# A one-core mixture-of-experts layer: residual placed in PSUM at the router, gate applied at the down-projection copies, gathers moved into gaps

## The chip, the cores and the metric

The kernel runs on one core of one Trainium2 chip, as one program. A core has a matrix engine (TensorE, PE in the rows; PEld is its weight load), VectorE (DVE), ScalarE (ACT), GpSimd (POOL) and SyncE (SP), which issues nearly all transfers here, and 16 DMA engines that move weights from HBM into SBUF. Matmuls write only into PSUM, which has eight banks of 512 fp32 columns. The metric is the device time of one execution in microseconds (us), as the median of several runs. The profile is of one execution.

## The reference

One transformer layer over 256 latent positions and 256 context positions of width 1024: a modulated RMS norm, a mixing stage (Fourier group, neighbourhood attention, short convolution, one output projection), then a mixture of experts with 32 experts of width 512, two per token out of one group of eight, and a final norm. What the change touches is the last part:

```python
x = x + g1 * mix_out(fx, attn_x, conv_x, w_fourier, w_out)
hx2 = rms_norm(x, norm2) * (1 + sc2) + sh2
y = hier_moe(hx2.reshape(-1, d), w_rg, b_rg, w_re, b_re, w_gate, w_up, w_down)
x = x + g2 * y.reshape(b, n, d)          # g2: one gate per column
return rms_norm(x, norm_final)
# in hier_moe, for every expert e:
he = jax.nn.silu(t @ w_gate[e]) * (t @ w_up[e])
y = y + combine[:, e:e + 1] * (he @ w_down[e])
```

## The kernel before

**Stages.** Up to about 175 us the mixing stage runs. Then the router (lines 781 to 836) computes logits, picks two experts per token, ranks tokens within each expert with five small matmuls (lines 829 to 832) and builds one-hot matrices. Then 32 experts follow in order, in eight groups of four. Up to 32 tokens of an expert (CAP) are computed; a branch (`overflow`, line 978) holds the rest.

**Weights.** Each expert has three transfers of 2 MB: `gu0`, `gu1` (the two halves of the contraction of gate and up) and `dn`. They land in slabs: ten in `slabs` and an eleventh, `more`, opened where the first stage's memory is closed (line 842). `pump` (line 123) issues the next transfers of a list on SyncE's queue as soon as the program order has a free slab; the transfer itself waits until the slab's last reader is done. `drop` gives a slab back: `gu0` and `gu1` of an expert within `hidden` (line 925), `dn` after the down projection (line 945). With eleven slabs, the transfer for `gu1` of expert 4 waits for `dn` of expert 0.

**One expert** (`expert`, line 954). `hidden` runs 32 gate/up matmuls in eight steps j (line 922; a matmul shows as two records, so 64), four for `gu0` and four for `gu1`. In step 7 `gather` (line 890) fetches the next expert's tokens: a one-hot matmul (line 897), a copy, two transposes (line 902), and the norm's gain and shift (line 906, VectorE). Then Silu (line 930, ScalarE), the product (line 932, VectorE), a transpose (line 934) and a copy. `project_down` (line 939) runs 16 matmuls (line 944) and copies the result into rows 32i of `yg`, four copies that alternate between VectorE and ScalarE (line 952). The next group's first gather is not in a step 7: it stands after `scatter`.

**Combine weights.** In the first expert, between `hidden` and `project_down`, `weights` (line 850) computes the two softmaxes' weights on VectorE and ScalarE. `weighted(g)` (line 878) multiplies a group's one-hot by them on GpSimd and transposes the result on TensorE (line 885). All engines run their own instructions in program order, so `project_down` stands behind this transpose on TensorE.

**Collecting.** `scatter(g)` (line 908) adds a group's four expert outputs into `yp`, four PSUM banks that hold the sum over all groups but the last, without the residual and without the gate g2.

**The end.** The last group is written out by hand (lines 1030 to 1075). The three gathers of experts 29 to 31 run ahead of expert 28. After its down projection VectorE multiplies `yp` by the gate and adds it to the residual `xs` (lines 1045, 1046, four times each). Identity matmuls (line 1053) put `xs` into four other banks, `py`. `group_add` (line 1069) adds experts 28 to 30 there, around the gate/up matmuls of expert 31. Then expert 31's output is added in five pieces, and the final norm and the store follow (lines 1100 to 1130). The last `gu1` comes in four pieces, the last `dn` in five.

Of the kernel before, what the change touches and what calls it, by code (L numbers as in the profile page):

```python
# [23 lines left out]
P = 128  # L24
# [53 lines left out]
def tile_kernel(ctx: ExitStack, tc: tile.TileContext, x, cx, small_a, small_b, b_g1, b_g2, w_ada, w_in, w_out, w_gu, w_dn, out):  # L78
# [746 lines left out]
    pr = [bank((P, NE)) for _ in range(3)]  # L825
    for fs in zip(route(0), route(1)):
        for f in fs:
            f()
    PE.matmul(pr[0], trib, msk[:, 0, :], start=True, stop=True)
    for i, first_ in ((1, trib), (2, onesb)):  # L830
        PE.matmul(pr[i], onesb, msk[:, 0, :], start=True, stop=False)
        PE.matmul(pr[i], first_, msk[:, 1, :], start=False, stop=True)
    for fs in zip(place(0, pr[0]), place(1, pr[1])):
        for f in fs:
            f()
    DVE.tensor_reduce(most, pr[2], axis=AX.X, op=OP.max)
    pro.close()
    over = keep.tile([P, 1], I32, name="over")
    ge = keep.tile([P, 2, NG], F32, name="ge")


# [7 lines left out]

    def weights():  # L850

        DVE.tensor_scalar(over, most, float(CAP), None, op0=OP.is_gt)
        for t in range(2):
            DVE.tensor_scalar(sm[:, t, 1:2], mg[:, t, 0:1], -1.0, None, op0=OP.mult)
            ACT.activation(ge[:, t, :], gl[:, t, 0:4], AF.Exp, bias=sm[:, t, 1:2], scale=1.0, accum_out=sm[:, t, 2:3])
        DVE.tensor_tensor(sm[:, :, 6:7], me[:, :, 1:2], me[:, :, 0:1], OP.subtract)
        ACT.activation(sm[:, :, 7:8], sm[:, :, 6:7], AF.Exp)
# [7 lines left out]
    yp = [mbank() for i in range(4)]  # L865
    state = {}
    onehots = {}

    def group(g):

        st = fst if g == 0 else onehot(g, mo.tile([P, 2, 4, CAP], F32, name="st"))
        onehots[g] = st
        sr = fsr if g == 0 else mo.tile([P, 2, 4, CAP], F32, name="sr")
        if g:
            DVE.tensor_tensor(sr, st, rr[:, :, None, None].to_broadcast([P, 2, 4, CAP]), OP.mult)
        state[g] = [mo.tile([P, 4, NJ, CAP], F32, name="xg", tag="xg"), None, None, sr]

    def weighted(g):

        st = onehots[g]  # L880
        sw = mo.tile([P, 2, 4, CAP], F32, name="sw", tag="sw")
        POOL.tensor_tensor(sw, st, cmb[:, :, 4 * g:4 * g + 4, None].to_broadcast([P, 2, 4, CAP]), OP.mult)
        pg = mbank((P, 2, P))
        for t in range(2):
            PE.transpose(pg[:, t, :], sw[:, t], ident)
        sl = mo.tile([P, 2, P], F32, name="sl", tag="sl")
        ACT.copy(sl, pg)
        state[g][1:3] = sl, mo.tile([P, D], F32, name="yg", tag="yg")

    def gather(e):  # L890

        g, i = divmod(e, 4)
        xg, sr = state[g][0], state[g][3]
        pg = mbank((P, 256))
        for t in range(2):
            for q in range(4):
                PE.matmul(pg[32 * q:32 * q + 32, :], sr[:, t, i, :], xs[:, t, blk(q, 256)], start=(t == 0), stop=(t == 1))  # L897
        gt = mo.tile([P, 256], F32, name="gt", tag="sw")
        (DVE.tensor_copy if e % 2 else ACT.copy)(gt, pg)  # L899
# [3 lines left out]
        dst = xg[:, i].rearrange("p (q c) n -> p c q n", c=2)  # L903
# [4 lines left out]
    def scatter(g):  # L908

        _, sl, yg, _ = state[g]  # L910
        for t in range(2):
            for h in range(2):
                PE.matmul(yp[2 * t + h], sl[:, t, :], yg[:, blk(h, 512)], start=(g == 0), stop=(g == NE // 4 - 2))  # L913

    def hidden(e, fill={}, work=None):
        g, i = divmod(e, 4)
        xg = state[g][0]
        wgu = [loaded[f"gu{h}", e].rearrange("p (s j f) -> p s j f", s=2, j=4) for h in range(2)]
        pg = mbank((P, 2, P))
        for j in range(NJ):  # L920
            for q in range(4):
                PE.matmul(pg[32 * q:32 * q + 32], xg[:, i, j, :], wgu[j // 4][:, :, j % 4, q * P:(q + 1) * P],  # L922
# [4 lines left out]
            for k in fill.get(j, ()):  # L927
                work(k)
# [3 lines left out]
        DVE.tensor_tensor(hh, pg[:, 1, :], sg, OP.mult)  # L932
        pt = mbank((P, P))
        PE.transpose(pt, hh, ident)  # L934
        ht = mo.tile([P, P], F32, name="ht", bufs=2)
        DVE.tensor_copy(ht, pt)
        return ht

    def project_down(e, ht, yg, i):
# [7 lines left out]
        for q in range(4):  # L947
            dst, src = yg[32 * i:32 * i + 32, blk(q, 256)], pd[32 * q:32 * q + 32, :]
            if e >= NE - 4:
                DVE.tensor_tensor(dst, src, g2b[32 * i:32 * i + 32, blk(q, 256)], OP.mult)  # L950
            else:
                (ACT.copy if q % 2 else DVE.tensor_copy)(dst, src)  # L952

    def expert(e):
        g, i = divmod(e, 4)
        ht = hidden(e, {NJ - 1: (e + 1,)} if i < 3 else {}, gather)
        if i == 0:
            if g == 0:
                weights()
            weighted(g)  # L960
        project_down(e, ht, state[g][2], i)

# [15 lines left out]
    def overflow():  # L978
# [3 lines left out]
        for t in range(2):  # L982
# [7 lines left out]
            for e in range(NE):  # L990
                gu = w_gu[e].rearrange("h p (s j f) -> p h s j f", s=2, j=4)
                dn = w_dn[e].rearrange("p (q k f) -> p q k f", q=4, k=4)
                for k in range(4):
# [10 lines left out]
                    for q in range(4):  # L1004
# [6 lines left out]
                        PE.matmul(yp[2 * t + q // 2][:, blk(q % 2, 256)], ident, y, start=False, stop=False)  # L1011

    fst = mo.tile([P, 2, 4, CAP], F32, name="st")
    group(0)
    gather(0)
    onehot(0, fst)
    for e in range(NE - 4):
        expert(e)
        g, i = divmod(e, 4)
        if i == 3:  # L1020
            scatter(g)
            if g == 3:
                n_over = nc.values_load(over[0:1, 0:1], min_val=0, max_val=1)
                with tc.If(n_over > 0):  # L1024
                    overflow()
# [192 lines left out]
```

## Time and profile before

| what | us |
|---|---|
| median of three runs (641.08 to 642.42) | 641.42 |
| the profiled execution's own time | 643.3 |
| its span, first to last instruction | 641.4 |
| TensorE busy | 486.1 (76%) |
| VectorE busy | 234.8 (37%) |
| ScalarE busy | 142.2 (22%) |
| 16 DMA engines, SyncE's queue | 92.1% of the span |
| mean rate of all transfers | 384 GB/s |
| mean granted TensorE clock | 0.917 |

All stages count into the shares. The rate over 40 slices and the rows of a stage tell more than a share of the whole. Chains and waits are inferred from semaphore events. Some matmul records can be missing.

### The profile page before, as it was taken

To read this page: it belongs to the slowest core of one execution; us is meant where nothing else is said; L and a number is where in the kernel's file an instruction comes from. 1 tells how busy PE (TensorE), PEld (TensorE's weight loads), DVE (VectorE), ACT (ScalarE), POOL (GpSimd) and SP (SyncE) were. 2 spreads that over 40 slices of the span, in tenths; PEclk is the share of its full clock that TensorE was granted. 3 is DMA by queue.
4 is the path that set the end of the run, shared out by engine and by line. 5 is a ranking of instruction groups with operands and counts; after the bars stand their busy time and mean duration, and the time that the engine had idled before them with its cause. 6 is when DMAs were issued, how large, how long until landed. Compare 5 with 4: busy or idle time off the path is not lost.

```text
span 641.4 us, 11767 instructions
## 1 busy us (share of the span) xinstructions
PE 486.1 (76%) x5133; PEld 294.5 (46%) x5133; DVE 234.8 (37%) x552; ACT 142.2 (22%) x319; POOL 10.3 (2%) x24
## 2 busy tenths in 40 slices
PE   3899999999966787777866665766766757578685
PEld 3788885856743344334423232432423333225342
DVE  5959785797642222222211111211211111122423
ACT  4564345756312111011101000101010000001003
POOL 1000000000000000000000000000000000000000
PEclk9999999999967889899889788987987898888798
DMA  8999973499997999999999999999999999999961
GB/s 344 424 424 407 394 300 131 145 376 396 391 391 298 429 425 427 425 425 424 427 427 424 427 425 419 426 425 428 425 424 426 427 427 427 425 427 424 420 230 65
DMA packets 21222, 246.16 MB, mean 384 GB/s; under 512 B 2214, under 2 KB 3242, under 8 KB 6956
## 3 DMA queue, kind: packets, MB, share of 16 engines
q1 hardware_dynamic: 21016, 245.08, 92.1%
q8 instruction: 42, 0.69, 0.4%
q10 hardware_dynamic: 148, 0.27, 0.1%
q14 instruction: 16, 0.13, 0.1%
HBM read 244.28 MB, written 1.05 MB: 383 GB/s over the span
## 4 chain that ended last, share of the span: by engine, by line
PE 46%; DMA 43%; DVE 7%; ACT 2%; issue 2%; POOL 0%; DVEq 0%; ACTq 0%; POOLq 0%; SPq 0%
DMA gu<-in_w_gu 24%; DMA dn<-in_w_dn 18%; PE b L524 12%; PE m L922 8%; PE m L944 5%; PE b L722 4%; PE m L897 2%; PE m L913 2%; PE b L664 1%; PE b L709 1%; DVE xg L906 1%; PE b L699 1%; DVE a L293 1%; PE b L310 1%; PE m L902 1%
## 5 line engine op out<-in xcount | busy, mean ns | idle before, releaser
L922 PE MATMUL m<-gu,xg 128*32 128x256 f32 x2048 | 132.1, 409 | 39.9 <-DMA gu<-in_w_gu 33.0
L922 PEld LDWEIGHTS m<-gu,xg 128*32 128x32 f32 x2048 | 70.8, 118 | 97.5 <-DMA gu<-in_w_gu 35.9
L944 PE MATMUL m<-dn,ht 128*32 128x256 f32 x992 | 82.3, 489 | 16.0 <-DMA dn<-in_w_dn 7.3
L944 PEld LDWEIGHTS m<-dn,ht 128*32 128x32 f32 x992 | 38.4, 136 | 47.8 <-issue 32.0
L952 DVE COPY yg<-m 32x256 f32<-32x256 f32 x56 | 23.4, 418 | 99.7 <-PE m L944 87.4
L952 ACT COPY yg<-m 32x256 f32<-32x256 f32 x56 | 20.4, 363 | 158.1 <-DVE yg L952 158.1
L524 PE MATMUL b<-uh,ws 128*128 128x256 f32 (+1 forms) x240 | 51.8, 306 | 0.0
L906 DVE TENSOR_TENSOR xg<-m,a 128x256 f32<-128x256 f32 x32 | 13.6, 425 | 83.0 <-PE m L902 83.0
L524 PEld LDWEIGHTS b<-uh,ws 128*128 128x128 f32 x240 | 39.1, 188 | 4.8 <-issue 2.8
L930 ACT ACTIVATE sg<-m 128x128 f32<-128x128 f32 x32 | 8.9, 278 | 125.3 <-PE m L922 125.3
L934 PE MATMUL m<-ident,hh 128*128 128x128 f32 x32 | 10.1, 314 | 35.1 <-DVE hh L932 35.1
L524 PE MATMUL b<-ul,ws 128*128 128x256 f32 (+1 forms) x120 | 35.8, 301 | 0.0
L899 DVE COPY gt<-m 128x256 f32<-128x256 f32 x16 | 6.8, 425 | 78.8 <-PE m L897 78.8
L897 PE MATMUL m<-xs,sr 128*32 128x256 f32 x448 | 31.7, 402 | 4.5 <-PEq L1024 4.5
L913 PE MATMUL m<-yg,sl 128*128 128x512 f32 x56 | 25.9, 605 | 6.5 <-ACT yg L952 6.5
L902 PE MATMUL m<-ident,gt 128*128 128x128 f32 x64 | 14.3, 307 | 19.0 <-DVE gt L899 10.8
L932 DVE TENSOR_TENSOR hh<-m,sg 128x128 f32<-128x128 f32 x32 | 9.1, 285 | 53.6 <-ACT sg L930 53.6
L495 ACT CAST ws<-in 128x1024 fp32r<-128x1024 f32 x20 | 21.0, 1049 | 33.2 <-PE b L524 30.7
L524 PE MATMUL b<-ws,uh 128*128 128x512 f32 (+1 forms) x96 | 26.2, 361 | 1.9 <-ACT uh L353 1.9
L722 PE MATMUL b<-ws,cat 128*128 128x512 f32 x96 | 27.4, 414 | 0.0
L500 DVE TENSOR_TENSOR ws<-in,ws 128x1024 fp32r<-128x1024 f32 x20 | 24.3, 1222 | 7.7 <-ACT ws L495 7.5
L934 PEld LDWEIGHTS m<-ident,hh 128*128 128x128 f32 x32 | 4.5, 140 | 45.2 <-issue 28.8
(249 smaller groups left out, 561.1 us busy)
## 6 DMA issues: line engine op xcount, KB each, us to landing
gu<-in_w_gu SPq DMA_DIRECT2D x63, 2048.0 KB, 39.2
dn<-in_w_dn SPq DMA_DIRECT2D x31, 2048.0 KB, 39.2
ada<-in_w_ada SPq DMA_DIRECT2D x12, 2048.0 KB, 12.6
in<-in_w_in SPq DMA_DIRECT2D x3, 2048.0 KB, 9.9
in<-in_w_in SPq DMA_DIRECT2D x8, 512.0 KB, 15.9
out<-in_w_out SPq DMA_DIRECT2D x2, 2048.0 KB, 9.5
gu<-in_w_gu SPq DMA_DIRECT2D x4, 512.0 KB, 28.5
dn<-in_w_dn SPq DMA_DIRECT2D x3, 512.0 KB, 11.5
```

The lines of the kernel that those rows point to most:

```text
L495: ACT.copy(ws[:, 0], loaded[kind, i][:, blk(c, 1024)])
L500: DVE.tensor_tensor(split[n][:, 1], loaded[kind, i][:, blk(c, 1024)], split[n][:, 0].bitcast(F32), OP.subtract)
L524: PE.matmul(po, st, mv, start=begins, stop=(c == 3 and tail and not any(po is v[1] for v in todo[n + 1:])))
L722: PE.matmul(held["yo", t, h], held["cat"][:, a, MIX[n], blk(t)], ws[:, b, h, :], start=(held["nm", t, h] == 0), stop=(held["nm", t, h] == ...
L897: PE.matmul(pg[32 * q:32 * q + 32, :], sr[:, t, i, :], xs[:, t, blk(q, 256)], start=(t == 0), stop=(t == 1))
L902: PE.transpose(pt[:, c], gt[:, blk(c)], ident)
L906: DVE.tensor_tensor(dst, src, w, op)
L913: PE.matmul(yp[2 * t + h], sl[:, t, :], yg[:, blk(h, 512)], start=(g == 0), stop=(g == NE // 4 - 2))
L922: PE.matmul(pg[32 * q:32 * q + 32], xg[:, i, j, :], wgu[j // 4][:, :, j % 4, q * P:(q + 1) * P], start=(j == 0), stop=(j == NJ - 1))
L934: PE.transpose(pt, hh, ident)
L944: PE.matmul(pd[32 * q:32 * q + 32, :], ht[:, 32 * k:32 * k + 32], wdn[:, q, k, :], start=(k == 0), stop=(k == 3))
L952: (ACT.copy if q % 2 else DVE.tensor_copy)(dst, src)
```

## The change

1. The four result regions `py` are opened at the router. Identity matmuls put the residual `xs` into them there, ahead of the five ranking matmuls. `yp` is gone: `scatter` adds straight into `py`.
2. The first stage's memory and banks are closed after the logits' first step, ahead of the rest of the routing.
3. The exponentials of the combine weights move to the router, as do two activations that load the tables of Exp and Silu. The rest of `weights` moves ahead of expert 0.
4. The gate g2 is laid out once (`g2q`, four one-row matmuls and a copy). The four copies after a down projection become four VectorE multiplications by it.
5. `gather` is cut in two: `gathered` (one-hot matmuls and the copy) runs after the gate/up matmuls, where Silu and the product are being computed; `placed` (transposes, gain and shift) runs after the hidden state's transpose. This holds at group borders too, but for expert 16, which stands behind the overflow branch.
6. `weighted` runs in a group's second expert, its transposes (`turned`) in the third; `scatter(g - 1)` runs in the first expert of group g. In the last group the update of `xs`, the late identity matmuls, the three early gathers and an extra one-hot product with its transposes are gone.

The diff, cut to its core:

```diff
+    routes = route(0), route(1)
+    for fs in routes:
+        fs.pop(0)()
     pro.close()
+    ACT.activation(sm[:, :, 3], zero.to_broadcast([P, 2]), AF.Exp)
...
+    py = {}
+    for a, b in ((0, 512), (512, 768), (768, 1024)):
+        whole = mbank((P, 2, 256)) if a else None
+        for t in range(2):
+            py[t, a, b] = whole[:, t, :] if a else mbank()
+            PE.matmul(py[t, a, b], ident, xs[:, t, a:b], start=(t == 0 or not a), stop=False)
+    pr = mbank((P, 3, NE))
+    for fs in zip(*routes):
+        for f in fs:
+            f()
+    PE.matmul(pr[:, 0, :], trib, msk[:, 0, :], start=True, stop=True)
...
+    for t in range(2):
+        DVE.tensor_scalar(sm[:, t, 1:2], mg[:, t, 0:1], -1.0, None, op0=OP.mult)
+        ACT.activation(ge[:, t, :], gl[:, t, 0:4], AF.Exp, bias=sm[:, t, 1:2], scale=1.0, accum_out=sm[:, t, 2:3])
+    DVE.tensor_tensor(sm[:, :, 6:7], me[:, :, 1:2], me[:, :, 0:1], OP.subtract)
+    ACT.activation(sm[:, :, 7:8], sm[:, :, 6:7], AF.Exp)
+    ACT.activation(sm[:, :, 3:4], sm[:, :, 6:7], AF.Silu)
...
-    yp = [mbank() for i in range(4)]
...
+        for (t, a, b), p in py.items():
+            PE.matmul(p, sl[:, t, :], yg[:, a:b], start=False, stop=False)
...
-            if e >= NE - 4:
-                DVE.tensor_tensor(dst, src, g2b[32 * i:32 * i + 32, blk(q, 256)], OP.mult)
-            else:
-                (ACT.copy if q % 2 else DVE.tensor_copy)(dst, src)
+            rows = blk(q, 32)
+            DVE.tensor_tensor(yg[blk(i, 32), blk(q, 256)], pd[rows, :], g2q[rows, :], OP.mult)
+
+    def upto(e):
...
+        return hidden(e, {NJ: [fetch], NJ + 1: [put]})
 
     def expert(e):
         g, i = divmod(e, 4)
-        ht = hidden(e, {NJ - 1: (e + 1,)} if i < 3 else {}, gather)
+        ht = upto(e)
+        if i == 2 and g < NE // 4 - 1:
+            group(g + 1)
         if i == 0:
-            if g == 0:
-                weights()
-            weighted(g)
+            if g not in (0, 4):
+                scatter(g - 1)
+            state[g][2] = mo.tile([P, D], F32, name="yg", tag="yg")
         project_down(e, ht, state[g][2], i)
+        if i == 1:
+            state[g][1] = weighted(g)
+        if i == 2:
+            pg = turned(g, state[g][1])
...
+    g2q = mo.tile([P, 256], F32, name="g2q")
...
     onehot(0, fst)
+    weights()
...
     gate_rows()
+    expert(NE - 3)
     gain_rows()
-    project_down(NE - 4, ht, yg, 0)
-    for t in range(2):
-        for h in range(2):
-            hs = blk(h, 512)
-            DVE.tensor_tensor(junk, yp[2 * t + h], g2b[:, hs], OP.mult)
-            DVE.tensor_tensor(xs[:, t, hs], xs[:, t, hs], junk, OP.add)
...
-    for k in (0, 1, 2):
-        group_add(k)
-    ht = hidden(e, {6: (3,), 7: (4, 5)}, group_add)
+    expert(NE - 2)
...
+    ht = hidden(e, {3: [partial(group_add, k) for k in (0, 1, 2)], 6: [partial(group_add, 3)], 7: [partial(group_add, k) for k in (4, 5)]})
```

## Rows read from the trace of the kernel before

**Rows 1.** The page, part 2: DMA engines' busy tenths and rate, 40 equal slices.

```profile
DMA  8999973499997999999999999999999999999961
...
GB/s 344 424 424 407 394 300 131 145 376 396 391 391 298 429 425 427 425 425 424 427 427 424 427 425 419 426 425 428 425 424 426 427 427 427 425 427 424 420 230 65
```

**Rows 2.** Timeline, SyncE's transfer issues, 190 to 210 us; columns: start, duration, operation, count.

```profile
191.55 0.33 SPq L152 DMA_DIRECT2D dn<-in_w_dn  x1
...
194.48 11.49 SPq L152 DMA_DIRECT2D gu<-in_w_gu  x2
```

**Rows 3.** Busy time by stretch, 202 to 208 us: PE, PEld, DVE, ACT, POOL, clock, DMA.

```profile
202.00:204.00 2.00, 2.00 (x21) 0.92 (x24) 0.00 (x0) 0.37 (x1) 0.00 (x0) 0.50 0.54 229
...
204.00:206.00 2.00, 2.00 (x24) 0.96 (x20) 0.35 (x1) 0.00 (x0) 0.00 (x0) 0.50 0.04 16
...
206.00:208.00 2.00, 2.00 (x30) 0.92 (x24) 0.48 (x2) 0.73 (x2) 0.00 (x0) 0.64 0.71 156
```

**Rows 4.** Timeline, TensorE and one VectorE row, router to first down projection; brackets: idle before.

```profile
177.16 2.87 PE L778 MATMUL b<-sa,x1t 128*128 128x40 f32 x24
...
180.07 0.26 DVE L788 SCALAR_TENSOR_TENSOR lg<-b,cst,lb 128x40 f32<-128x40 f32 x1 [1.29 <-PE b L778]
...
182.22 0.19 PE L829 MATMUL b<-msk,trib 128*128 128x32 bf16 x1 [2.19 <-DVE msk L796]
...
183.71 1.94 PE L897 MATMUL m<-xs,fsr 128*32 128x256 f32 x16 [1.12 <-DVE cst L836]
...
187.85 6.56 PE L922 MATMUL m<-gu,xg 128*32 128x256 f32 x64 [0.98 <-DVE xg L906]
...
201.33 0.69 PE L885 MATMUL m<-ident,sw 128*128 128x128 f32 x2 [3.48 <-POOL sw L882]
...
201.95 3.64 PE L944 MATMUL m<-dn,ht 128*32 128x256 f32 x32
```

**Rows 5.** Timeline, TensorE, one scatter and two neighbouring experts, 236 to 262 us.

```profile
236.19 3.70 PE L913 MATMUL m<-yg,sl 128*128 128x512 f32 x8 [0.93 <-ACT yg L952]
...
252.21 3.66 PE L922 MATMUL m<-gu,xg 128*32 128x256 f32 x64
...
255.67 1.07 PE L897 MATMUL m<-xs,sr 128*32 128x256 f32 x16
...
261.42 3.64 PE L922 MATMUL m<-gu,xg 128*32 128x256 f32 x64
```

**Rows 6.** Timeline, the last group's residual update and the last gate/up matmuls.

```profile
593.99 0.69 DVE L1045 TENSOR_TENSOR fin<-m,fin 128x512 f32<-128x512 f32 x1
...
599.44 4.27 PE L1053 MATMUL m<-xs,ident 128*128 128x512 f32 x9
...
624.85 0.64 PE L922 MATMUL m<-gu,xg 128*32 128x256 f32 x8
```

**Rows 7.** Last weights: issues, median us to landing (page and 594 to 598 us), DMA end.

```profile
gu<-in_w_gu SPq DMA_DIRECT2D x63, 2048.0 KB, 39.2
...
572.61 0.33 SPq L152 DMA_DIRECT2D gu<-in_w_gu  x1
...
592.17 5.60 SPq L150 DMA_DIRECT2D gu<-in_w_gu  x1
...
gu<-in_w_gu SPq DMA_DIRECT2D x1, 512.0 KB, 25.0
...
620.00:622.00 2.00, 2.00 (x32) 1.13 (x34) 0.00 (x0) 0.00 (x0) 0.00 (x0) 1.00 0.42 116
```

**Rows 8.** Timeline, TensorE: two gate/up halves after a wait for their transfer.

```profile
497.50 3.62 PE L922 MATMUL m<-gu,xg 128*32 128x256 f32 x32 [2.00 <-DMA gu<-in_w_gu]
...
542.67 1.93 PE L922 MATMUL m<-gu,xg 128*32 128x256 f32 x32 [2.10 <-DMA gu<-in_w_gu]
```

**Rows 9.** The copies out of the down projection: the page's group, and the last group's.

```profile
L952 DVE COPY yg<-m 32x256 f32<-32x256 f32 x56 | 23.4, 418 | 99.7 <-PE m L944 87.4
...
592.20 1.76 DVE L950 TENSOR_TENSOR yg<-m,fin 32x256 f32<-32x256 f32 x4 [7.03 <-PE m L944]
```

More of the change, by code (lines that the diff above doesn't have):

```diff
@@ L885, in weighted, with gathered @@
             PE.transpose(pg[:, t, :], sw[:, t], ident)
[L886 to L893, printed above, removed]
+        state[g][1] = mo.tile([P, 2, P], F32, name="sl", tag="sl")
+        ACT.copy(state[g][1], pg)
+        return pg
+    def gathered(e):
         pg = mbank((P, 256))
@@ L908, in scatter, with hidden @@
     def scatter(g):
-        _, sl, yg, _ = state[g]
-        for t in range(2):
-            for h in range(2):
[L913 to L917, printed above, removed]
+        _, sl, yg = state[g]
+        for (t, a, b), p in py.items():
+            PE.matmul(p, sl[:, t, :], yg[:, a:b], start=False, stop=False)
+    def hidden(e, between={}):
         wgu = [loaded[f"gu{h}", e].rearrange("p (s j f) -> p s j f", s=2, j=4) for h in range(2)]
@@ L926, in hidden @@
                 pump()
-            for k in fill.get(j, ()):
-                work(k)
+            for f in between.get(j, ()):
+                f()
         sg = mo.tile([P, P], F32, name="sg", tag="sg", bufs=2)
@@ L1010, in overflow, with tokens @@
                         DVE.tensor_scalar(y, pd, late[:, t, e:e + 1], None, op0=OP.mult)
-                        PE.matmul(yp[2 * t + q // 2][:, blk(q % 2, 256)], ident, y, start=False, stop=False)
+                        pd = mbank((P, 256), "f")
+                        PE.matmul(pd, ones[32 * q:32 * q + 1, :], rg[32 * q:32 * q + 1, :], start=True, stop=True)
+                        DVE.tensor_tensor(y, y, pd, OP.mult)
+                        p = py[(t, 0, 512) if q < 2 else (t, 256 * q, 256 * q + 256)]
+                        PE.matmul(p[:, blk(q, 256)] if q < 2 else p, ident, y, start=False, stop=False)
+    def tokens():
+        return mo.tile([P, 4, NJ, CAP], F32, name="xg", tag="xg")
     fst = mo.tile([P, 2, 4, CAP], F32, name="st")
+    xg = tokens()
     group(0)
-    gather(0)
+    placed(0, gathered(0))
+    g2q = mo.tile([P, 256], F32, name="g2q")
+    pq = mbank((P, 256))
+    for q in range(4):
+        PE.matmul(pq[blk(q, 32), :], ones[32 * q:32 * q + 1, 0:32], rg[32 * q:32 * q + 1, :], start=True, stop=True)
+    ACT.copy(g2q, pq)
     onehot(0, fst)
+    weights()
     for e in range(NE - 4):
         expert(e)
[L1019 to L1025, printed above, removed]
-            group(g + 1)
-            gather(e + 1)
-    g = NE // 4 - 1
-    weighted(g)
-    _, sl, yg, _ = state[g]
-    for i in (1, 2, 3):
-        gather(NE - 4 + i)
-    ht = hidden(NE - 4)
+        if e == 15:
+            scatter(3)
+            n_over = nc.values_load(over[0:1, 0:1], min_val=0, max_val=1)
+            with tc.If(n_over > 0):
+                overflow()
+            xg = tokens()
+            placed(e + 1, gathered(e + 1))
+    g = NE // 4 - 1
+    expert(NE - 4)
     fin = take("fin")
@@ L1039, in tile_kernel @@
     gate_rows()
+    expert(NE - 3)
     gain_rows()
[L1041 to L1063 removed]
+    expert(NE - 2)
+    _, sl, yg = state[g]
     e = NE - 1
```

86 lines of the change are left out of this document (37 added, 49 removed).

## The prediction, made before the changed kernel was run

> **What bounds the kernel now.** I read the rate of transfers first. From about 208 us to 610 us the DMA engines are busy and move 419 to 429 GB/s [rows 1], and nothing in the change makes a transfer smaller. So TensorE work between these times has no price of its own; what counts is where the stream stops and what is left when it ends. At 80 to 130 us it is low as well, but the change touches nothing there.
>
> The stop is at 202 to 208 us: the DMA share is 0.54, 0.04 and 0.71 in three stretches of 2 us [rows 3], idle time of (0.46 + 0.96 + 0.29) x 2 = 3.4 us. SyncE's row shows why: it issues two transfers from 194.48 on, and the second gets out only after 11.49 us, at 206.0 [rows 2]. That is `gu1` of expert 4, which needs the slab of `dn` of expert 0, and expert 0's down projection ran from 201.95 to 205.6 [rows 4]. Two things make it late. Expert 0's gate/up matmuls took 6.56 us [rows 4] where the same 64 records take 3.66 later on [rows 5], and the one-hot matmuls before them 1.94 (16 records) against 1.07: the granted clock was at its lower level (1.2 GHz). And TensorE stood idle for 3.48 us in front of the transposes of line 885 [rows 4], since the combine weights weren't ready.
>
> At the other end TensorE runs behind the stream. The last quarter of `gu1` of expert 31 was issued at 592.17 and landed 25.0 us later, at 617.2 [rows 7]; its matmuls start at 624.85 [rows 6], 7.65 us after. The check: `gu0` of expert 31, issued at 572.61, lands by the median of 39.2 us at 611.8, and a 2 MB transfer takes 4.9 us at 426 GB/s, so its `gu1` is in by about 617; the stream runs out at 620 to 622 [rows 7]. From 624.85 to the end of the span are 16.55 us of a chain that the change leaves as it is.
>
> **Part by part: the router.** The residual's identity matmuls stream 2 x 512 + 4 x 256 = 2048 columns, as a scatter does, which takes 3.70 us at the higher clock [rows 5]; at the lower clock it would be 7.4, and nine of the twelve records of line 1053 took 4.27 us there [rows 6]. They stand behind the last logits matmul, which ends at 180.03. Their banks are free when the last logits are read, at 180.33 at the latest [rows 4]. Before, TensorE waited from 180.03 to 182.22 for VectorE's routing, so 2.2 us of them are hidden. The ranking matmuls stand behind them: they move from 182.22 to 184.0, a loss of 1.8 us, or up to 5.5 at the lower clock. I take the former, since TensorE was busy without a gap until 180.03 [rows 4] and now has no pause there.
>
> Then the five ranking matmuls, VectorE's placing and the one-hot matmuls follow as before: 183.71 - 182.22 = 1.5 us later the gather starts [rows 4], at 185.5. If the clock holds it takes 1.07 instead of 1.94. The way from the gather's end to the gate/up matmuls was 187.85 - 185.65 = 2.2 us, with transposes at the lower clock; I take 2.0. Expert 0 starts at 188.6, 0.7 us later than before, but ends its gate/up matmuls at 192.2 against 194.4. No wait for combine weights follows: their last VectorE steps are done beside these matmuls. Of the gap's work (gather of expert 1 1.07, transposes) I count 2 us, then 1.9 for the down projection. `dn` of expert 0 is free at about 196.2 instead of 205.6. The stream runs dry at about 203 [rows 3], and 0.7 us pass between the issue at 206.0 and the flow. So there are some 6 us to spare, and even with all of it at the lower clock (start 192, gate/up 6.6, 3.3 in the gap, 3.6) it is free at 205.5, which is as before. **The stop of 3.4 us goes.** By bytes (229 + 16 + 156 GB/s where 426 was possible) it is 4.1; I take 3.4, as packets under way at the restart are counted late. All later landings come 3.4 us earlier.
>
> Closing the first stage's memory earlier moves the eleventh slab in program order only: its transfer waits for the last reader, the logits matmuls, either way. I cost it at nothing; 0 to 1 us would be covered by the queue that is full then.
>
> **The middle.** One expert takes 261.42 - 252.21 = 9.2 us of TensorE's time [rows 5], against 3 x 4.92 = 14.8 us of its transfers. Each edit is inside the 5.6 us between: the gathers in the gap hide 1.07 us behind Silu and the product (a gain that the wait for the next weights swallows); the four copies by VectorE alone take 1.76 us as multiplications [rows 9], 0.44 each, where VectorE's copies took 0.42 [rows 9] and alternated with ScalarE one after the other; the scatter, now behind the next group's first gate/up matmuls, puts 3.70 us ahead of that expert's down projection, so its slab comes free 3.7 us later, with eight transfers queued ahead. ScalarE loses half of these copies, which frees nothing that others wait for. All cost 0.
>
> **The end.** Gone from TensorE's way are eight VectorE operations at 0.69 us [rows 6], 5.5 us, the identity matmuls, 4.27 us of which followed them [rows 6], and the burst of early gathers. So TensorE can follow the landings. `gu0` of expert 31 is in at 611.8 - 3.4 = 608.4. Its 32 records take 1.93 us at the higher clock and 3.62 at the lower; after a wait of 2 us both happen [rows 8]. Then three group additions, now 512 + 512 + 256 columns: 1280/2048 x 3.70 = 2.3 us. Steps 4 to 6 take 3 x 0.48, the addition in step 6 0.46. So the last step starts at 608.4 + 1.93 + 2.3 + 1.45 + 0.46 = 614.5, or at 616.2 with the first half at the lower clock; the piece itself is in at 617.2 - 3.4 = 613.8, so TensorE sets it by 0.7 to 2.4 us. I take 615.2, between the two, since both clocks occur after such a wait. The last `dn` piece is in by about 622 - 3.4 = 618.6 and is wanted 7.5 us after that step starts, later than it lands. End of the span: 615.2 + 16.55 = 631.8 us.
>
> **A rule against it.** In the end of before the clock stood at its higher level (1.00 at 620 to 622 [rows 7]), with TensorE busy and behind; after the change it waits for transfers in the last expert. [...]
>
> **The rivals.**
> (1) *Cold end.* The last expert from `gu0` on at 1.2 GHz: 608.4 + 3.6 + 4.6 + 2.9 + 0.9 = 620.4 for the last step, less what the clock regains while TensorE is then busy without a gap; with the final chain slower by 1 us at most half of it holds: about 635. For it: the waits. Against: after 608 TensorE has hardly a pause.
> (2) *The stop stays.* Identity matmuls at the lower clock and a cold expert 0 free `dn` at 205.5, as worked out: 631.8 + 3.4 = 635.2. Against: TensorE is warm when they start.
> (3) *No gain at the end.* The landing at 617.2 is one row; were the last `gu1` quarter in only when the stream ends (622), the slack would be 2.9 us instead of 7.65, giving 641.4 - 3.4 - 2.9 = 635.1; with the stop kept too, 638.5. If the residual's update had not been what the last expert waited for, the same.
> (4) *Slower.* The gap's serial order (gate/up, gather, transpose, copy, transposes, down projection) with three rotating banks makes an expert longer than its transfers. The point is 14.8 us. At the higher clock matmuls are 3.66 + 1.07 + 0.44 + 0.30 + 1.93 = 7.4 of the 9.2 us; all at the lower clock it would be 16.6 us, 1.8 over, and over 28 experts some 50 us more: about 690. Just past the point, at 14.9 to 15.2, the loss eats the gain of 9.6 us and the time is 642 to 645. Against: matmul busy time leaves 5.6 us of air, and TensorE catches up with the stream in before [rows 5, 8].
>
> **How the numbers follow.** The three runs' median, 641.42, is equal to the profiled span, 641.4; that execution's own time, 643.3, is 1.9 above. Gains are taken off the median: 641.42 - 3.4 - 6.2 = 631.8 (on the profiled execution 633.7). Chances: forecast 0.70, (1) 0.10, (2) 0.07, (3) 0.09, (4) 0.04. Lower end: 4.1 us for the stop, no lateness of TensorE: 641.4 - 4.1 - 7.65 = 629.6, and 0.6 for the landing read from one row: 629.0. Upper end: rivals 1 to 3, 635.2, and the clock's share: 636.0. Differences of 0.2% (1.3 us) are what a measurement of this kernel can tell. Of (3) a third ends near no change: same 0.04, slower 0.04, faster 0.92.
>
> **What would show it.** In the changed profile: no stretch around 202 to 208 us with a low DMA share; expert 0's gate/up matmuls in about 3.7 us and starting near 188.6; identity matmuls at 180.3 to 184; the down projection of expert 0 done by about 197; experts 28 to 31 each waiting for a transfer; the last gate/up step at 614 to 616, and 16 to 17 us behind it. The prediction is wrong if the stop stays, if TensorE still doesn't wait for transfers in the last group, or if the final chain grows beyond 18 us at the lower clock.

## The result and the profile after

The changed kernel took 635.62 us (633.13 to 636.62) against 641.92 for the kernel before in the same set: a ratio of 0.989 [0.986, 0.993], a gain of 6.3 us where 9.6 were forecast. Two more sets of the same file gave 634.71 against 642.53, 0.988 [0.985, 0.991], and 634.39 against 641.16, 0.988 [0.986, 0.991]. The profiled execution took 636.62 us; its span is 634.8, beside a span of 641.4 before.

The rate of transfers comes first: page of the changed kernel, part 2, 40 equal slices, to be laid beside [rows 1].

```profile
DMA  9999983399999999999999999999999999999981
GB/s 358 418 423 405 392 320 132 134 355 393 392 390 381 427 424 424 427 424 428 422 427 427 426 427 422 422 424 425 427 426 425 425 426 427 425 427 424 422 309 70
```

The slice that had 298 GB/s has 381. The stretches of [rows 3], in the changed kernel (busy us of PE, PEld, DVE, ACT, POOL, then granted clock, DMA share, GB/s):

```profile
202.00:204.00 2.00, 1.87 (x30) 1.14 (x34) 1.02 (x3) 0.08 (x1) 0.00 (x0) 1.00 1.01 422
204.00:206.00 2.00, 2.00 (x44) 1.19 (x40) 1.46 (x4) 0.00 (x0) 0.00 (x0) 1.00 0.98 418
206.00:208.00 2.00, 2.00 (x44) 1.23 (x40) 0.22 (x1) 0.05 (x1) 0.00 (x0) 1.00 1.02 434
```

The stop is gone. TensorE's way from the router to the first down projection (timeline of the changed kernel; beside [rows 4]):

```profile
180.35 5.41 PE L846 MATMUL m<-xs,ident 128*128 128x512 f32 x12 [0.35 <-DVE lg L788]
185.59 0.18 PE L851 MATMUL m<-msk,trib 128*128 128x32 bf16 x1
...
186.87 1.07 PE L905 MATMUL m<-xs,fsr 128*32 128x256 f32 x16 [1.00 <-DVE fsr L823]
...
189.96 3.66 PE L932 MATMUL m<-gu,xg 128*32 128x256 f32 x64 [0.46 <-PE m L1063]
...
195.33 1.93 PE L958 MATMUL m<-dn,ht 128*32 128x256 f32 x32
```

The residual's matmuls (line 846) took 5.41 us, not 3.70: in the windows at 180 to 182 and 182 to 184 us the granted clock is 0.62 and 0.52. The ranking matmuls therefore come 3.4 us later than before. All the same the down projection is done at 197.3, since the rest runs at the higher clock and no wait for weights is left.

The end (timeline of the changed kernel, beside [rows 6]; brackets show the wait):

```profile
564.70 1.93 PE L932 MATMUL m<-gu,xg 128*32 128x256 f32 x32 [2.79 <-DMA gu<-in_w_gu]
571.05 3.64 PE L932 MATMUL m<-gu,xg 128*32 128x256 f32 x32 [4.42 <-DMA gu<-in_w_gu]
...
610.39 3.53 PE L932 MATMUL m<-gu,xg 128*32 128x256 f32 x32 [2.31 <-DMA gu<-in_w_gu]
613.85 2.46 PE L1095 MATMUL m<-yg,sl 96*128 96x512 f32 x6
...
618.31 0.64 PE L932 MATMUL m<-gu,xg 128*32 128x256 f32 x8
```

TensorE now waits for transfers in the last group, so it follows the stream instead of running behind it. The last gate/up step starts at 618.31, where 615.2 was forecast, and 634.8 - 618.31 = 16.5 us stand behind it, as forecast (16.55). Of the 3.1 us, 2.0 are there when `gu0` of expert 31 lands, at 610.39 instead of 608.4; the other 1.1 are mostly its matmuls at the lower clock, 3.53 us, where I had taken a value between the two levels.

SyncE's issues tell the pace of landings, as it gets a transfer out when an earlier one is in (the issue at 571.07 beside the wait that ends at 571.05). Timeline of SyncE, changed kernel:

```profile
559.71 0.33 SPq L152 DMA_DIRECT2D gu<-in_w_gu  x1
564.62 0.33 SPq L152 DMA_DIRECT2D dn<-in_w_dn  x1
571.07 0.33 SPq L152 DMA_DIRECT2D gu<-in_w_gu  x1
```

The steady step is 4.90 us. Here one is 6.45: a landing is 1.55 us late, while the DMA share stays at 1.00 from 566 to 572 us. In this profile that happens at 228, 347, 442 and 571 us, and at 403, where the next step makes it up; in the profile before, with about 1.05 us each, at 314, 409 and 528. So the issue of `gu0` of expert 31, at 572.61 [rows 7], comes 1.54 us earlier and not 3.4.

### The profile page after: what moved, and what is told of

Read it like the earlier page. It is cut to its first block, busy times and chain, and to the rows that moved or that the text cites. A ratio compares the mean times of both kernels' runs of the same rounds, so it can differ in the third digit from the quotient of the medians.

```text
span 634.8 us, 11800 instructions
## 1 busy us (share of the span) xinstructions
PE 484.0 (76%) x5167; PEld 298.1 (47%) x5167; DVE 247.7 (39%) x587; ACT 128.0 (20%) x281; POOL 9.1 (1%) x20
## 3 DMA queue, kind: packets, MB, share of 16 engines
HBM read 244.28 MB, written 1.05 MB: 386 GB/s over the span
## 4 chain that ended last, share of the span: by engine, by line
DMA 63%; PE 32%; DVE 3%; issue 1%; ACT 1%; DVEq 0%; SPq 0%; ACTq 0%
DMA gu<-in_w_gu 44%; DMA dn<-in_w_dn 18%; PE b L524 12%; PE b L722 4%; PE m L932 3%; PE b L664 1%; PE b L709 1%; PE b L699 1%; DVE a L293 1%; PE b L310 1%; PE m L958 1%; PE m L846 1%; PE m L1115 1%; PE m L1095 1%; PE m L905 1%
## 5 line engine op out<-in xcount | busy, mean ns | idle before, releaser
L932 PE MATMUL m<-gu,xg 128*32 128x256 f32 x2048 | 153.7, 454 | 100.8 <-DMA gu<-in_w_gu 98.9
L963 DVE TENSOR_TENSOR yg<-m,g2q 32x256 f32<-32x256 f32 x124 | 52.1, 420 | 62.4 <-PE m L958 61.0
L958 PE MATMUL m<-dn,ht 128*32 128x256 f32 x992 | 61.6, 389 | 11.8 <-DMA dn<-in_w_dn 11.7
L958 PEld LDWEIGHTS m<-dn,ht 128*32 128x32 f32 x992 | 31.6, 111 | 33.3 <-DVE xg L918 11.4
L905 PE MATMUL m<-xs,fsr 128*32 128x256 f32 x512 | 40.1, 436 | 5.3 <-PEq L1072 4.3
L905 PEld LDWEIGHTS m<-xs,fsr 128*32 128x32 f32 x512 | 19.4, 128 | 21.5 <-issue 13.1
L924 PE MATMUL m<-yg,sl 128*128 128x256 f32 (+1 forms) x84 | 25.4, 451 | 1.0 <-DVE yg L963 1.0
L524 PEld LDWEIGHTS b<-ul,ws 128*128 128x128 f32 x120 | 22.4, 188 | 0.9
L722 PEld LDWEIGHTS b<-ws,cat 128*128 128x128 f32 x96 | 16.5, 188 | 7.5 <-issue 4.1
L907 ACT COPY gt<-m 128x256 f32<-128x256 f32 x31 | 11.5, 372 | 41.6 <-PE m L905 41.6
## 6 DMA issues: line engine op xcount, KB each, us to landing
gu<-in_w_gu SPq DMA_DIRECT2D x63, 2048.0 KB, 39.2
dn<-in_w_dn SPq DMA_DIRECT2D x31, 2048.0 KB, 39.2
ada<-in_w_ada SPq DMA_DIRECT2D x12, 2048.0 KB, 12.4
```

The costliest lines, as they stand in the source:

```text
L524: PE.matmul(po, st, mv, start=begins, stop=(c == 3 and tail and not any(po is v[1] for v in todo[n + 1:])))
L722: PE.matmul(held["yo", t, h], held["cat"][:, a, MIX[n], blk(t)], ws[:, b, h, :], start=(held["nm", t, h] == 0), stop=(held["nm", t, h] == ...
L905: PE.matmul(pg[32 * q:32 * q + 32, :], fsr[:, t, e % 4, :], xs[:, t, blk(q, 256)], start=(t == 0), stop=(t == 1))
L907: (DVE.tensor_copy if e == 0 else ACT.copy)(gt, pg)
L924: PE.matmul(p, sl[:, t, :], yg[:, a:b], start=False, stop=False)
L932: PE.matmul(pg[32 * q:32 * q + 32], xg[:, e % 4, j, :], wgu[j // 4][:, :, j % 4, q * P:(q + 1) * P], start=(j == 0), stop=(j == NJ - 1))
```

## The experiments

Theory A of the expectations is mine: front and end each gain by themselves, the router's delay is covered, and what is missing is late landings and the clock of the last half. Its rivals are named there for each run. Kernels of one set share the runs of the kernel before; line numbers are those of each kernel, so the changed kernel's line 932 can be 934 or 936.

**The changed kernel again.** No edit; it asks whether the late landings stay where they were.

> The changed kernel as it is, once more. Its first profile ended at 634.8 us where 631.8 was predicted: the last gate and up halves landed only 1.5 us earlier than before instead of 3.4, after one transfer came 1.55 us late at 571 us. Theory A (the stream of weights makes pauses of about 1.55 us now and then, at places that differ between executions, and the end meets one more or one fewer): ratio to the kernel before 0.985 to 0.991, and in this profile the late transfers stand at other times than 347, 403, 442 and 571 us. Theory B (the change itself makes one transfer late): a late transfer at 571 us again.

634.71 against 642.53, 0.988 [0.985, 0.991]; span 632.6. Timeline of its TensorE:

```profile
608.34 3.43 PE L932 MATMUL m<-gu,xg 128*32 128x256 f32 x32 [2.57 <-DMA gu<-in_w_gu]
...
616.11 0.64 PE L932 MATMUL m<-gu,xg 128*32 128x256 f32 x8
```

Late landings are at 301, 401 and 520 us, one fewer than in the first profile up to 572 (without its made-up one at 403), and `gu0` of expert 31 is in at 608.34: the forecast's 608.4. With the half at the lower clock the last step starts at 616.11, the forecast's 616.2 for that case. So the sum holds to 0.1 us where the late landings fall as they do here, and their places belong to the execution, not to the change.

**The front alone.** The kernel before with the combine weights computed ahead of expert 0.

```diff
         if i == 0:
-            if g == 0:
-                weights()
             weighted(g)
...
     onehot(0, fst)
+    weights()
+    ACT.activation(sm[:, :, 3:4], sm[:, :, 6:7], AF.Silu)
```

> The kernel before with one part of the change: the combine weights are worked out before expert 0, so that expert 0's down projection has no wait of 3.5 us in front of it. All else is as before. Theory A (the stop of the stream at 202 to 208 us is set by when that down projection ends): it ends at about 202 to 203 instead of 205.6, the stop shrinks from 3.4 to below 1 us, and all later landings come earlier; the end, which stays bound by TensorE, follows: 638.0 to 640.0 us against 641.9. Theory B (the stop costs nothing at the end, since TensorE is behind the stream there): 641 to 642.5.

640.24 against 642.53, 0.997 [0.995, 0.999], so 2.3 us (0.2 us outside the time expected, against a kernel before that was 0.6 us slower in this set); span 638.5 instead of 641.4. Timeline of its TensorE:

```profile
188.30 5.21 PE L922 MATMUL m<-gu,xg 128*32 128x256 f32 x64 [0.98 <-DVE xg L906]
...
197.47 1.93 PE L944 MATMUL m<-dn,ht 128*32 128x256 f32 x32 [0.17 <-DVE ht L936]
...
621.96 0.64 PE L922 MATMUL m<-gu,xg 128*32 128x256 f32 x8
```

`dn` is free at 199.4 instead of 205.6 though gate/up still ran mostly at the lower clock; the DMA share at 202 to 208 us is 1.06, 0.97 and 0.96. This edit is enough to remove the stop. Of the 6.2 us, 3.6 are won between gate/up and the down projection, where the wait stood [rows 4], 1.7 in the down projection (1.93 us instead of 3.64, at the higher clock), and 0.9 as gate/up ends earlier. The end moved by 624.85 - 621.96 = 2.9 us with its long chain unchanged.

**The residual behind expert 0.** The changed kernel with only these matmuls moved.

```diff
-            PE.matmul(py[t, a, b], ident, xs[:, t, a:b], start=(t == 0 or not a), stop=False)
+    def residual():
+        for (t, a, b), p in py.items():
+            PE.matmul(p, ident, xs[:, t, a:b], start=(t == 0 or not a), stop=False)
...
         expert(e)
+        if e == 0:
+            residual()
```

> The changed kernel with the residual's six identity matmuls moved from the router to behind expert 0. Theory A (they delay expert 0 by 3.4 us, but that is covered, as long as its down projection ends before the stream runs dry at 203): expert 0's gate and up matmuls start near 186.5 but run at the lower clock (6.6 us), its down projection ends between 197 and 201, no stop appears, and the time is that of the changed kernel within 0.3%. Theory B (the delay at the router is paid at the end): 3 us faster than the changed kernel.

633.84, 0.987 [0.983, 0.990], beside 0.988 for the changed kernel. Timeline of its TensorE:

```profile
182.79 0.21 PE L855 MATMUL m<-msk,trib 128*128 128x32 bf16 x1 [2.19 <-DVE msk L796]
...
188.30 5.66 PE L936 MATMUL m<-gu,xg 128*32 128x256 f32 x64
...
195.69 1.93 PE L962 MATMUL m<-dn,ht 128*32 128x256 f32 x32
...
610.10 1.93 PE L936 MATMUL m<-gu,xg 128*32 128x256 f32 x32 [2.63 <-DMA gu<-in_w_gu]
...
616.38 0.64 PE L936 MATMUL m<-gu,xg 128*32 128x256 f32 x8
```

The router is 2.8 us faster and expert 0's matmuls 2.0 us slower, so the down projection starts at 195.69 instead of 195.33: behind TensorE's work at the router they run at the higher clock, without it mostly at the lower. It makes no difference in time that the intervals tell. In its last expert, after a wait of 2.63 us, the half took 1.93: the last step is at 616.38, with `gu0` as late as 610.10.

**The front undone.** The residual's matmuls behind expert 0, as in the run just shown, and the combine weights back between hidden state and down projection of expert 0. So it differs from the run just shown in the combine weights alone.

```diff
+            if g == 0:
+                weights()
+                turned(0, weighted(0))
         project_down(e, ht, state[g][2], i)
-        if i == 1:
+        if i == 1 and g:
             state[g][1] = weighted(g)
...
     onehot(0, fst)
-    weights()
```

> The changed kernel with its front undone: the residual's matmuls behind expert 0 and the combine weights with their transposes between expert 0's hidden state and its down projection, as in the kernel before. The end is that of the changed kernel. Theory A (front and end are two separate gains): the down projection of expert 0 ends at 204 to 206, the stop of 2 to 3.4 us is back, and the time is 1.5 to 3.4 us above the changed kernel, 637 to 639. Theory B (all of the gain is at the end): the same as the changed kernel, within 0.2%, with the stop in the trace. Theory C (all of it is at the front): 641 to 642.

636.58, 0.991 [0.988, 0.995]: 1.9 us over the changed kernel of this set and 2.7 us over the run with the residual behind expert 0 (633.84). The intervals of the ratios overlap, so each of these is good to a us or two. The stretches again, in this kernel:

```profile
202.00:204.00 2.00, 2.00 (x25) 0.72 (x17) 0.00 (x0) 0.40 (x1) 0.00 (x0) 0.58 0.59 246
204.00:206.00 2.00, 2.00 (x9) 1.02 (x6) 1.67 (x4) 0.00 (x0) 0.00 (x0) 1.00 0.67 147
206.00:208.00 2.00, 2.00 (x16) 1.43 (x18) 0.00 (x0) 0.00 (x0) 0.00 (x0) 1.00 0.90 360
```

The idle share is (0.41 + 0.33 + 0.10) x 2 = 1.7 us, and on TensorE the wait is back: its timeline has

```profile
200.10 0.58 PE L897 MATMUL m<-ident,sw 128*128 128x128 f32 x2 [4.08 <-POOL sw L891]
```

A stop of 1.7 us costs 1.9 to 2.7. It is half the old stop, as the down projection is done at 204.0 and not 205.6. This kernel gains 642.53 - 636.58 = 6.0 us, but not by the end alone, as half of the stop is gone here too. Less those 1.7 us, the end alone is worth about 4.3 (an estimate); with 2.3 for the front alone that is 6.6, beside 7.8 for both. Front and end each gain, but no run has the end alone beside the whole stop, and that the two add up is not shown closer than this.

**Order of work in the last wait: three runs.** (a) the final norm's gain rows one expert later, (b) the first three group additions ahead of expert 31, where TensorE waits, (c) both.

```diff
     expert(NE - 3)
-    gain_rows()
     expert(NE - 2)
+    gain_rows()
...
+    for k in (0, 1, 2):
+        group_add(k)
-    ht = hidden(e, {3: [partial(group_add, k) for k in (0, 1, 2)], 6: ..., 7: ...})
+    ht = hidden(e, {6: ..., 7: ...})
```

> The changed kernel with the sixteen matmuls of the final gain rows moved from before expert 30 to between expert 30 and expert 31, where TensorE waits some 2.3 us for the first half of the last gate and up weights. Nothing else moves. Theory A (after this wait the first half runs at the lower clock in some executions, 3.5 us instead of 1.93, and this is paid in full at the end): with TensorE busy there, the half takes 1.93 us and the last step starts 5.9 to 6.4 us after the half's landing, as in the run with the residual late (610.10 to 616.38), not 7.8 (608.34 to 616.11): 0 to 1.6 us below the changed kernel, 633 to 635. Theory B (the last step is set by its own weights landing): no change beyond 0.3 us, with a wait for a transfer in front of the last step.

> The changed kernel with the first three group additions (1280 columns) moved from behind the first half of expert 31's gate and up matmuls to in front of it, into the same wait. Theory A (TensorE's own work of 6.3 to 7.8 us between the landing of that half and the last step sets the end, and the last quarter lands before): additions of the first 512 columns start as soon as two of the four copies are done, the last step starts 5.5 us after the landing or less: 1 to 2.5 us below the changed kernel. Theory B (the last quarter's landing sets it): within 0.3 us.

> Both of these: gain rows and then the first three group additions between expert 30 and the first half of expert 31. Together they are 4.5 us of work for a wait of 2.3, so the half starts late, but at the higher clock. Theory A: last step 5.5 to 6.3 us after the landing of the half, 1 to 2 us below the changed kernel, no more than the additions alone give. Theory B (the landing sets it): within 0.3 us.

Against 641.91: (a) 635.27, 0.988 [0.985, 0.991]; (b) 633.28, 0.985 [0.982, 0.989]; (c) 634.04, 0.985 [0.982, 0.988]. Timeline of TensorE with (a), late landings at the places of the first profile:

```profile
609.88 1.16 PE L1003 MATMUL m<-ident,sa 128*128 128x128 f32 x8 [0.59 <-DVE yg L963]
611.59 1.93 PE L932 MATMUL m<-gu,xg 128*32 128x256 f32 x32 [0.56 <-ACT fin L996]
...
617.86 0.64 PE L932 MATMUL m<-gu,xg 128*32 128x256 f32 x8
```

The half ran at the higher clock, but began about 1 us after the piece was in (issued at 571.30; 39.3 us later, as in the first profile, would be 610.6, an estimate), as the rows waited for VectorE and ScalarE. Of the 1.6 us that the clock gave, these waits took 1.0: the last step starts 7.3 us after the landing, where 5.9 to 6.4 were expected and the changed kernel has 7.9, and the medians don't tell the rest. With (b):

```profile
608.38 2.39 PE L1095 MATMUL m<-yg,sl 96*128 96x512 f32 x6 [0.69 <-DVE yg L963]
610.70 2.80 PE L932 MATMUL m<-gu,xg 128*32 128x256 f32 x48
613.82 0.64 PE L932 MATMUL m<-gu,xg 128*32 128x256 f32 x8 [0.33 <-DMA gu<-in_w_gu]
...
615.15 0.64 PE L932 MATMUL m<-gu,xg 128*32 128x256 f32 x8
```

The additions lie in the wait and the steps behind run at the higher clock. The last quarter of `gu1`, issued at 590.14, lands 25.0 us later, at 615.1; its step starts at 615.15. In the changed kernel it is in at 590.63 + 25.0 = 615.6 and used at 618.31, 2.7 us later. With (b) the stream, not TensorE, sets the end. With (c) the rows delay the additions, and the last step is at 616.11.

**The serial update put back beside the rest.** In the changed kernel, ahead of expert 29, the residual's update is done into a scratch bank that nothing reads.

```diff
     gate_rows()
+    for t in range(2):
+        for h in range(2):
+            hs = blk(h, 512)
+            DVE.tensor_tensor(junk, xs[:, t, hs], g2b[:, hs], OP.mult)
+            DVE.tensor_tensor(junk, junk, xs[:, t, hs], OP.add)
+            PE.matmul(mbank(), ident, junk, start=True, stop=True)
     expert(NE - 3)
```

> The changed kernel with the removed update put back as work without effect on the result: after the gate rows, four times a VectorE multiplication and an addition of 512 columns each followed by an identity matmul of 512 columns into a scratch bank that waits for them. Theory A (what the end gained is this serial stretch, and TensorE has some 5 us of waits for transfers between expert 29 and expert 31 to take it up): VectorE needs 5.5 us, TensorE is held for 7 to 9 us at expert 28, catches up by expert 30, and the end is 0 to 4 us later than the changed kernel. Theory B (the stretch never was on the path, and the gain comes from the gathers and the clock): no change within 0.3 us, with the waits for transfers of expert 30 and 31 as long as in the changed kernel.

639.13, 0.995 [0.992, 0.997]; by the ratios 4.3 us over the changed kernel of the second and third sets. Timeline of its TensorE:

```profile
582.36 2.04 PE L1089 MATMUL m<-fin,ident 128*128 128x512 f32 x2 [0.84 <-DVE fin L1088]
...
595.34 5.35 PE L932 MATMUL m<-gu,xg 128*32 128x256 f32 x64
...
620.26 0.64 PE L932 MATMUL m<-gu,xg 128*32 128x256 f32 x8
```

TensorE is held from 582.36 to 595.3, and after that no gate/up half waits for a transfer: it is behind the stream again, as before. So serial work at this place does reach the end. But the stretch put back is longer than the one taken out. VectorE in this run, then the last of its steps in the kernel before (which begin at 593.99 [rows 6]):

```profile
580.80 0.69 DVE L1087 TENSOR_TENSOR fin<-xs,fin 128x512 f32<-128x512 f32 x1
...
584.51 0.69 DVE L1087 TENSOR_TENSOR fin<-xs,fin 128x512 f32<-128x512 f32 x1 [2.30 <-PE m L1089]
...
592.53 0.69 DVE L1088 TENSOR_TENSOR fin<-fin,xs 128x512 f32<-128x512 f32 x1
```

```profile
599.07 0.69 DVE L1046 TENSOR_TENSOR xs<-xs,fin 128x512 f32<-128x512 f32 x1
```

Here `junk` is one buffer that the matmul reads, so the next multiplication waits for it: 12.4 us in all, beside 5.8 in the kernel before. The 4.3 us are therefore no measure of what the old update cost; how the end's gain divides between the update, the identity matmuls and the early gathers is not shown.

**More instructions.** The late landings needed a cause. In the trace, 16 KB packets of the queue of kind "instruction" run beside the weights; one takes 1.1 us of one engine (568 to 570 us: 3.5% of 16 engines in 2 us, and 571.07 is a late landing). This run adds 64 small matmuls ahead of each of experts 4 to 27, into a scratch bank.

```diff
+    def pad():
+        scratch = mbank((P, NE), "f")
+        for _ in range(64):
+            PE.matmul(scratch, trib, msk[:, 0, :], start=True, stop=True)
...
+        if 4 <= e < 28:
+            pad()
```

> The changed kernel with 64 small bf16 matmuls (32 columns, into a scratch bank that nobody reads) in front of each of the experts 4 to 27, some 3000 instructions more on TensorE, placed where it waits for weights. The data moved for the kernel is the same; only the fetch of instructions grows, some 190 KB in packets of 16 KB. Theory A (the transfers that land 1.1 to 1.6 us late in every profile, at places that differ, are due to instruction fetches on the same DMA engines): more of them than the three or four between 300 and 600 us of the other runs, six or more, and the time rises by 2 to 8 us. Theory B (they have nothing to do with instructions): three or four of them, and the time of the changed kernel within 0.3%.

636.68 against 641.16, 0.993 [0.990, 0.995], 2.3 us over the changed kernel of this set. Page, part 3, of this kernel, then of the changed kernel:

```profile
q8 instruction: 55, 0.90, 0.6%
```

```profile
q8 instruction: 43, 0.70, 0.4%
```

Between 250 and 600 us late landings are at 278, 363, (405), 428, 503 and 598 us, five in place of three beside the one near 400 (six or more were expected), and `gu0` of expert 31 is issued at 572.20 instead of 570.79. The packets between two late landings, counted by windows of the changed kernel (345 to 441, 441 to 570 us) and of the padded one (357 to 425, 425 to 502), transfers by queue:

```profile
q8 instruction: 8, 0.13, 0.6%
...
q8 instruction: 8, 0.13, 0.4%
```

```profile
q8 instruction: 8, 0.13, 0.8%
...
q8 instruction: 8, 0.13, 0.7%
```

Eight each time, at intervals of 95 to 129 us in the one and 65 to 95 in the other. The same count stands between the late landings of the kernel before (314, 409, 528), of the third profile of the changed kernel (318, 417, 541) and of (a) and (b) above. Those near 403 us, at the branch behind expert 15, are apart from it: they are mostly made up by the next step. In the second profile the eighth packet falls there too, at 401 us, and the next step makes nothing up. In two kernels (the front undone, the serial update) a late landing is split over smaller steps, and the count is less sharp there. So in these profiles a landing is late at every eighth instruction packet, and with more instructions it is late more often. Why the eighth isn't settled. The lengths of these packets in the trace repeat with a period of eight as well: in the changed kernel, from 281 us on, 1.02, 1.07, 1.07, 1.06, 1.10, 1.11, 1.09 and 1.02 us, and the next eight the same to 0.01. That the packets go round over eight engines, so that each eighth meets an engine that already had one, would fit both; the trace doesn't name the engine.

**The gather back in step 7.**

```diff
-        return hidden(e, {NJ: [fetch], NJ + 1: [put]})
+        return hidden(e, {NJ - 1: [fetch, put]})
```

> The changed kernel with the next expert's gather put back into the last gate and up step, all of it ahead of Silu, as the kernel before had it, with the rest of the change kept. Theory A (the place of the gather is hidden by the wait for weights but for expert 0 and expert 30): the time of the changed kernel within 0.3%, with an expert some 1.4 us longer on TensorE. Theory B (the gathers in the gaps are a part of the gain): 1 us or more slower.

635.42, 0.990 [0.987, 0.993], 1.0 us over the changed kernel, which the intervals don't separate. Waits of TensorE from 300 to 560 us (us in total, times, longest), here, then in the changed kernel:

```profile
PE m L932 <- DMA gu<-in_w_gu: 34.9, 17, 4.0
PE m L946 <- DVE hh L942: 22.3, 18, 1.3
```

```profile
PE m L932 <- DMA gu<-in_w_gu: 66.5, 29, 4.0
...
PE m L946 <- DVE hh L942: 0.7, 1, 0.7
```

The gap's work takes 21.6 us of waits for the product away and turns up as 31.6 us more of waits for weights: real on TensorE, worth nothing in the middle. At the end the slack is smaller: `gu0` of expert 31 is waited for by 0.53 us only.

**Both moved, and the changed kernel a third time.** The residual behind expert 0 and the additions ahead of expert 31, the two edits above together.

> The changed kernel with two edits that were tried alone: the residual's matmuls behind expert 0, and the first three group additions ahead of expert 31's gate and up matmuls. In the run with the additions alone the last step started as its weights landed (615.15 us), so the stream sets the end. Theory A: the time of that run, ratio to the kernel before 0.983 to 0.987, 1 to 2 us below the changed kernel. Theory B (the earlier start of expert 0 adds a gain of its own): 3 us or more below the changed kernel.

> The changed kernel once more, beside the last three on the same chip. Ratio to the kernel before 0.985 to 0.991. In its profile the last step of expert 31 starts 5.9 to 7.9 us after the first half of that expert's weights landed, by the clock of that half.

633.09 (632.80 to 633.33), 0.987 [0.984, 0.989], beside 634.39 (632.86 to 636.38), 0.988 [0.986, 0.991], for the changed kernel. The intervals overlap; the medians differ by 1.3 us. The nine times of this kernel and of (b) lie between 632.1 and 634.2, the sixteen of the changed kernel between 632.9 and 636.6. Timeline of TensorE, both moved:

```profile
610.25 2.80 PE L936 MATMUL m<-gu,xg 128*32 128x256 f32 x48
613.38 0.64 PE L936 MATMUL m<-gu,xg 128*32 128x256 f32 x8 [0.33 <-DMA gu<-in_w_gu]
...
614.71 0.64 PE L936 MATMUL m<-gu,xg 128*32 128x256 f32 x8
```

Its last quarter was issued at 588.14 and took 26.5 us: in at 614.64, used at 614.71, so the stream sets the end here too. The 1.5 us over the 25.0 of the other profiles are again a late landing, eight packets after the one at 471 us. In the changed kernel's third profile `gu0` landed at 610.11, the half took 3.62 and the last step started at 618.06: the first profile once more.

## Why the prediction was right and where it was not

What held. The stop went, and alone is worth 2.3 us (the front alone), or 1.9 to 2.7 when half of it is put back. Expert 0's gate/up matmuls took 3.66 us (forecast 3.7), its down projection was done at 197.3 (about 197). TensorE waits for transfers in the last group, and with serial work put back there it falls behind them again and loses 4.3 us; which of the parts taken out counted most is not shown. The three additions took 2.46 us (2.3), the chain behind the last step 16.5 (16.55). Multiplications out of PSUM took 0.42 us each (0.44), and the middle is covered, as the waits for weights show: 66.5 us of air in 260. Two signs named beforehand did not come as named: in the first profile the last step started at 618.31 and not at 614 to 616, and of experts 28 to 31 the gate/up matmuls of expert 29 ran without a wait.

What was mis-sized. First, "All later landings come 3.4 us earlier". The stop is as long as forecast, but a landing is late by 1.5 us at every eighth instruction packet, and whether one more of these falls before the last transfers differs from run to run of the same kernel: the issue of `gu0` of expert 31 came 1.5 us earlier in the first profile, 3.6 in the second and 1.8 in the third. The term is 3.4 less 0 or about 1.6. I had compared one profile with itself and taken its landings as fixed. In [rows 7] the row with 39.2 us, a median of 63 transfers, doesn't show a late one; the list of issues does.

Second, the choice between the two clock levels for the last half (615.2 from 614.5 and 616.2). In all three profiles of the changed kernel it took 3.43 to 3.62 us, so 616.2 was the value to take. The rival "cold end", with the whole last expert slow, is not what came, as the steps behind the half ran at the higher clock, and in two other kernels (the residual behind expert 0, more instructions) the half itself took 1.93 after a wait of 2.6 us. The Trainium skill (TensorE: Matmul & The Clock Gate, section "Why this matters for your kernels") warns of long idle gaps between matmul bursts, after which the clock goes back to half. The waits here are shorter than the gaps it warns of, and the half still took 3.53 us after one of 2.31, so this trace does not agree with it.

Together: 631.8 + 2.0 (landing, 610.39 for 608.4) + 1.0 (the half at the lower clock) = 634.8, the span measured. The range held, by 0.4 us in the first set: its upper end came from rivals that did not come and from the clock. No term in it was a late landing, so that it covers one is in part luck.

Third, a step that was wrong and cost nothing: "now has no pause there". The residual's matmuls had the clock fall under them, and the ranking matmuls came 3.4 us later instead of 1.8, inside the bound of 5.5 given. With the delay taken away (the residual behind expert 0) the time is the same to 0.9 us in 634, within the noise. The prediction's bound for `dn`, 205.5 with all of it at the lower clock, would not have made the step safe: by its own terms expert 0 would start at 187.7 + 1.5 + 1.94 + 2.2 = 193.4 and not at 192, and `dn` would be free at 206.9, later than before. What made it safe is that in the first profile the clock was back at 1.00 from 184 us on, so the gather took 1.07 us and gate/up 3.66.

The rivals. The stop didn't stay. "No gain at the end" didn't come: about 4 us came from there. "Slower" needed an expert of more than 14.8 us; TensorE's waits for weights grew instead. Of "cold end" a first part came, 1.0 us.

One possibility wasn't weighed: that once the end follows the landings, the order of work inside the last wait decides. Additions ahead of the wait bring the last step to the landing of its piece (615.15 and 615.1).

## What to carry to other kernels

When a kernel is bound by a stream of transfers, read two things: where the stream stops, and how long after the last landing the last user starts. Each is a gain of its own, and work between them is only worth the air it leaves at the end. Put work that is ready ahead of the last wait, not behind it (1.3 to 1.4 us here by medians whose intervals overlap; the traces show the step 2.7 us nearer to its landing), and when a forecast goes by landings, take their times from the list of all issues and from more than one execution, since a late one moves the end by 1.5 us.

## What the runs showed of the hardware

Instruction loading shares the DMA engines with the weights: 43 packets of 16 KB in this kernel, 1.1 us of one engine each, and with each eighth a 2 MB transfer lands about 1.5 us late (6.45 us instead of 4.90 between issues; 5.95 in the kernel before) though the DMA share stays at 1.00. 1536 more matmuls made it 55 packets and two more late landings between 250 and 600 us.

The clock fell under work without a real pause: 1.00 at 178 to 180 us, 0.62 and 0.52 in the next two stretches, with 0.35 us of idle time between the logits' matmuls (40 columns each) and the residual's (256 and 512 columns). After waits of 2.3 to 2.7 us in the last expert the next 32 matmul records ran mostly at the lower clock in four profiles (3.22 to 3.62 us) and at the higher in two (1.93). What decides between them stays open.
